# A regrouped last down group, the mixer's values ahead of its first weights, and a fourth raw weight buffer in a fp32-by-three-products encoder kernel

## The chip, the cores and the metric

The kernel runs on one core of one Trainium2 chip. The metric is the device time of one execution in microseconds (us), as the median of several runs. One core has a tensor engine (PE), a vector engine (DVE), an activation engine (ACT), GpSimd (POOL) and a sync engine (SP), which here issues most of the loads and stores. Each engine works through its own instructions in order; semaphores tie them together.

## The reference

One encoder layer over 768 tokens (a sample of 512, "S", and a prompt of 256, "P") of width 1024, in float32:

```python
x = layer_norm(a * x + 0.5 * swiglu(x, ffn1_w_gu, ffn1_w_down))
x = layer_norm(a * x + parallel_mixer(x, ...))
x = layer_norm(a * x + memory_cross_attention(x, mem, ...))
x = layer_norm(a * x + 0.5 * swiglu(x, ffn2_w_gu, ffn2_w_down))
```

`swiglu` is `(silu(x @ gate) * (x @ up)) @ down` with an inner width of 2816. The mixer projects x to a short-convolution branch, to q, k, v and gates of a bidirectional gated linear attention with four heads, to a low-rank decay, and to two sigmoid gates that merge the branches. Attention is over 256 memory rows.

## The kernel before

**Products.** Every float32 operand is split into a rounded high part (ACT, `activation` with Copy, line L87) and a low part, the source minus the high part (DVE or POOL, L88). A product is then three matmuls: high by high, low by high, high by low (L106 to L108, or L335). Weights pass through `raw` tiles (128 x 1024 float32, 512 KB), loaded by SP and split into `wh` and `wl`. The tag `raw` has three buffers in the pool `wp`, `wh` and `wl` have five each. A load into a `raw` buffer waits until the splits and sums that read its former content are done.

**Order.** The code is written against a tile layer whose scheduler places the instructions of each engine; it need not keep the order of the program text. The pools decide which instruction waits for which, since a new tile takes the buffer of an older one. So a change in the text or in a ring moves instructions elsewhere too.

**The FFN** (`ffn_fast`, twice). The inner width is 22 blocks of 128. A block needs a gate and an up weight tile, and its result, of 128 x 768, is split into a tile `hq`. FFN1 begins with two plain blocks (`front1`), FFN2 with three; the others go through `seven`: the block is a 2 x 2 product of halves, done in seven products rather than eight (a Strassen–Winograd scheme). `seven.weights` loads the two tiles `rg` and `ru` and forms four sums of their halves on DVE (tag `tt`, L312 to L320) and their splits; `seven.products` runs the seven products on the PE (psum tiles `px`, `py`, `pz`), copies three partial results out (`snap`, ACT, L340) and adds three others (`sum`, DVE, L345). The PE's next product into `px` waits for that copy or sum. Behind them, silu (ACT, L401) and the gating multiply (DVE, L402) give the hidden block. In the start of FFN1 and in the mixer, `sums` forms the activation sums S1 to S4 with four scratch tiles from the snap ring; in the mixer the rings for `tt` and `snap` are unused pieces of another tile.

**Down.** The hidden blocks are stored to DRAM (`hspill`) except the last four, and come back in pairs: a pair of inner blocks is one weight tile for each half of the output columns. A group (`down_group`) accumulates its pairs over all six token tiles in psum (`dn`) and adds the result to `acc` (DVE, L213). The last group (`down_last`) goes tile by tile, first two tiles together, then one after another, for both column halves, and each tile's layer norm (`norm`, L134 to L177) follows while the PE is at the next tile. `hr` tiles, six of them, hold the hidden blocks that come back. FFN1 has the groups [9,10,0], [1,2,3], [4,5,6] and last [7,8]; FFN2 has [9,10,0], [1,2,3], [4,5] and last [6,7,8].

**Mixer start.** After LN1 the tokens are transposed on the PE (`lt`) and split to `xh` and `xl`; `lr` is the low-rank product, `pt` the q and k projections with four weight tiles, `values(range(3))` the v projection of three token tiles (`tb`, four weight tiles from w_v), and then ten pairs go through `seven`, the first two with weights w_g, the others with w_mix. `weights_of(*pairs[0][:2])` comes before `values(range(3))` in the text.

Of the kernel before, what the change touches and what calls it, by code (L numbers as in the profile page):

```python
# [7 lines left out]
F32 = mybir.dt.float32  # L8
# [50 lines left out]
def _encoder(ctx, tc, nc, io, out, dbg):  # L59
# [21 lines left out]
    def nid(p):  # L81
        uid[0] += 1
        return f"{p}{uid[0]}"
# [181 lines left out]
    HT = TT // 2  # L265
# [11 lines left out]
        ap_ = glob["accp"].enter_context(tc.tile_pool(name="accp", bufs=1, reuse_waits="tile"))  # L277
        glob["acc"] = ap_.tile([128, 6, D], F32, name="acc")

    def seven(X, tt, snap_t, sum_t):  # L280

        unit = [None, None, 2]

        def operand(src, eng):

            if unit[2] == 2:
                unit[0] = wp.tile([128, 1024], F32R, tag="wh", bufs=5, name=nid("wh"))
                unit[1] = wp.tile([128, 1024], F32R, tag="wl", bufs=5, name=nid("wl"))
                unit[2] = 0
            c = slice(unit[2] * 512, unit[2] * 512 + 512)  # L290
            unit[2] += 1
            h, l = unit[0][:, c], unit[1][:, c]
            split(h, l, src, eng)
            return h, l

        lo, hi = slice(0, 512), slice(512, 1024)

        def weights(wg, wu):

            rg, ru = [wp.tile([128, 1024], F32, tag="raw", bufs=3, name=nid("raw")) for _ in range(2)]  # L300
            for r, w in ((rg, wg), (ru, wu)):
                if len(w.shape) == 4:
                    r4 = r[:].rearrange("p (a b c) -> p a b c", a=4, b=2)
                    for z in range(2):
                        nc.sync.dma_start(r4[:, :, z, :], w[:, :, z, :])
                else:
                    nc.sync.dma_start(r[:], w)
            V, G = nc.vector, nc.gpsimd
            t = [tt() for _ in range(4)]
            b = {}  # L310
            b["P1"] = operand(rg[:, lo], V)
            V.tensor_tensor(t[0], rg[:, lo], ru[:, lo], op=ALU.add)  # L312
            b["P5"] = operand(t[0], V)
            V.tensor_tensor(t[1], t[0], ru[:, hi], op=ALU.add)
            b["P6"] = operand(t[1], V)
            b["P3"] = operand(ru[:, hi], G)
            V.tensor_tensor(t[2], ru[:, lo], ru[:, hi], op=ALU.add)
            b["P7"] = operand(t[2], V)
            b["P2"] = operand(rg[:, hi], G)
            V.tensor_tensor(t[3], t[1], rg[:, hi], op=ALU.add)  # L320
            b["P4"] = operand(t[3], V)
            return b

        LEFT = {"P1": "A11", "P2": "A12", "P3": "S4", "P4": "A22", "P5": "S1", "P6": "S2", "P7": "S3"}

        def product(p, b, ps, start):
            tiles(X[LEFT[p]], b[p], ps, start)

        def tiles(a, w, ps, start, ks=range(4)):
            (ah, al), (wh, wl) = a, w  # L330
            for k in ks:
                c = slice(k * 128, (k + 1) * 128)
                st, sp_ = start and k == 0, k == 3
                for n, (l, r) in enumerate(((wh, ah), (wh, al), (wl, ah))):
                    nc.tensor.matmul(ps, l[:, c], r[:, k, :], start=st and n == 0, stop=sp_ and n == 2,  # L335
                                     skip_group_check=True)

        def snap(ps, nm):
            t = snap_t()
            nc.scalar.activation(t, ps, AF.Copy)  # L340
            return t

        def added(ps, t, nm):
            o = sum_t()
            nc.vector.tensor_tensor(o, t, ps, op=ALU.add)  # L345
            return o

        def products(b):

            x = psum(nid("px"))[:, :HT]  # L350
            product("P1", b, x, True)
            p1 = snap(x, "p1")
            y = psum(nid("py"))[:, :HT]
            product("P5", b, y, True)
            p5 = snap(y, "p5")
            product("P6", b, x, False)
            u2 = snap(x, "u2")
            product("P3", b, y, False)
            up1 = added(y, u2, "up1")
            product("P7", b, x, False)  # L360
            up2 = added(x, p5, "up2")
            z = psum(nid("pz"))[:, :HT]
            product("P2", b, z, True)
            g1 = added(z, p1, "g1")
            product("P4", b, x, False)
            return g1, x, up1, up2

        return operand, weights, tiles, products, (lo, hi)

    def ffn_fast(n, i, front, order6, src, groups, last):  # L370
# [7 lines left out]
        X = {}  # L378
# [6 lines left out]
        def scratch(tag, n, bufs):  # L385
            return lambda: fp.tile([128, n], F32, tag=tag, bufs=bufs, name=nid(tag))[:]

        tt, snap_t = scratch("tt", 512, 4), scratch("snap", HT, 6)
        operand, weights_of, tiles, products, (lo, hi) = seven(X, tt, snap_t, scratch("sum", HT, 4))

        def weights(j):
            return weights_of(wgu[j], wgu[NFB + j])
# [89 lines left out]
    def mixer(i):  # L482
# [72 lines left out]
        def ring(own, n):  # L555
# [7 lines left out]
        X = {nm: tuple(sa.tile([128, 4, HT], F32R, name=f"m{nm}{p}") for p in "hl") for nm in ("S1", "S2", "S3", "S4")}  # L563
        quarters(X)
        snap_t = ring(slots[4:9], HT)
        _, weights_of, _, products, _ = seven(
            X, ring(slots[0:4], 512), snap_t,
            lambda: fx.tile([128, HT], F32, tag="sum", bufs=4, name=nid("sum"))[:])

        def big(nm):  # L570
            return fx.tile([128, TT], F32, tag="big", bufs=3, name=nid(nm))
# [1 line left out]
        for k in range(4):  # L573
            a = []
            for q in (k, k + 4):
                x = big("x0")
                nc.vector.tensor_tensor(x[:], xh["all"][:, q, :].bitcast(F32), xl["all"][:, q, :].bitcast(F32),
                                        op=ALU.add)
                a.append(halves(x))
            sums(X, snap_t, k, *a)  # L580

        def w_g(c):
            return io["w_g"].rearrange("a p (b c) -> p a b c", b=2)[:, :, :, c * 128:(c + 1) * 128]

        pairs = [(w_g(2 * c), w_g(2 * c + 1), AF.Silu, silud, 2 * c) for c in range(2)]
        pairs += [(wm[16 + 2 * c], wm[17 + 2 * c], AF.Sigmoid, sigd, 2 * c) for c in range(8)]
        ws = weights_of(*pairs[0][:2])
        values(range(3))
        for n, (_, _, fn, dst, c) in enumerate(pairs):
            g1, x, u1, u2 = products(ws)  # L590
            first, second = big("first"), big("second")
# [430 lines left out]
    def front1(env):  # L1022

        X, hp, fp = env["X"], env["hp"], env["fp"]
        plain_weights, plain_block = env["plain_weights"], env["plain_block"]
        env["open_A"](("A11", "A12", "A22", "S1", "S2", "S3", "S4"))
        V, G = nc.vector, nc.gpsimd
        ip_ = ExitStack()
        ip = ip_.enter_context(tc.tile_pool(name="start", bufs=1, reuse_waits="tile"))
        X["A21"] = tuple(ip.tile([128, 4, HT], F32R, name=f"A21{p}") for p in "hl")  # L1030
        x0 = [hp.tile([128, 2, TT], F32, tag="hq", bufs=4, name=nid("x0")) for _ in range(4)]

        def part(k):
            r4 = x0[k % 4][:, k // 4, :].rearrange("p (a two b) -> p a two b", two=2, b=128)
            return r4[:, :, 0, :], r4[:, :, 1, :]

        def first(k):
            nc.sync.dma_start(x0[k % 4][:, k // 4, :], io["xT"][k, :, :])
            for nm, src in zip((("A11", "A21"), ("A12", "A22"))[k // 4], part(k)):
                put(X[nm], k % 4, src, V)  # L1040

        w0 = plain_weights(0)
        plain_block(0, w0, first)
        w1 = plain_weights(1)
        for k in range(4):
            sums(X, env["snap_t"], k, part(k), part(k + 4))
        plain_block(1, w1)
        ip_.close()
        return 2, env["weights"](2)
# [2 lines left out]
        h, l = [t[:, k, :].rearrange("p (a b) -> p a b", b=128) for t in x]  # L1052
        split(h, l, src, eng)

    def sums(X, snap_t, k, a1, a2):
        V, G = nc.vector, nc.gpsimd
        (a11, a21), (a12, a22) = a1, a2
        s_ = [snap_t().rearrange("p (a b) -> p a b", b=128) for _ in range(4)]
        V.tensor_tensor(s_[0], a22, a21, op=ALU.subtract)
        put(X["S1"], k, s_[0], V)  # L1060
        V.scalar_tensor_tensor(s_[1], s_[0], -1.0, a11, ALU.mult, ALU.subtract)
        put(X["S2"], k, s_[1], V)
        V.scalar_tensor_tensor(s_[2], s_[1], -1.0, a12, ALU.mult, ALU.subtract)
        put(X["S4"], k, s_[2], G)
        V.tensor_tensor(s_[3], a11, a21, op=ALU.subtract)
        put(X["S3"], k, s_[3], V)
# [9 lines left out]
    def front2(env):  # L1076
# [24 lines left out]
        for k in range(4):  # L1101
            x0 = hp.tile([128, 2, TT], F32, tag="hq", bufs=4, name=nid("x0"))
            for eng, s in ((nc.gpsimd, S), (nc.vector, P)):
                eng.tensor_tensor(x0[:, :, s.cols], *[d["all"][:, k:NK:4, s.cols].bitcast(F32) for d in (xh, xl)],
                                  op=ALU.add)
            a = [[x0[:, c, h * HT:(h + 1) * HT].rearrange("p (a b) -> p a b", b=128) for h in range(2)]
                 for c in range(2)]
            sums(X, env["snap_t"], k, *a)
        w3 = env["weights"](3)
        for j in range(2):  # L1110
            env["gated"](j, h01[j], nc.vector)
        env["plain_block"](2, w2)
        return 3, w3

    ffn_fast(1, 0, front1, [0, 2, 4, 1, 3, 5], io["x_tok"], ([9, 10, 0], [1, 2, 3], [4, 5, 6]), [7, 8])
    mixer(1)
    x3 = dp.tile([128, 6, D], F32, name="x3")
    with tc.tile_pool(name="lnx", bufs=1) as lp, tc.tile_pool(name="xa", bufs=1, reuse_waits="tile") as ap:
# [128 lines left out]
```

## Time and profile before

| what | value |
|---|---|
| runs shown | median 1860.47 us (1858.65 to 1863.38) |
| profiled execution | 1864.59 us |
| its span, first to last instruction | 1862.7 us |
| PE busy | 1810.8 us, 97% |
| DVE, ACT, POOL busy | 1039.0, 716.2, 616.7 us |
| mean granted clock | 0.990 |

By the trace the stages lie as follows, in us from the span's start: the first two FFN1 blocks 0 to 61, its other blocks to 341, FFN1's down groups and LN1 about 348 to 543, the start of the mixer to 612, its pairs to 758, the rest of the mixer and the cross attention to about 1356, the start of FFN2 to 1398, its blocks to 1660, its down groups and LN to the end.

How to read the lines: a group of instructions is given with its source line, its engine and its tiles (output from inputs). A wait is "engine, tile, line, releaser: total, times, longest". A window row has the busy time and the count of instructions of each engine, then the granted PE clock (1.00 is full), the share of the DMA engines and the GB/s. In a timeline row the first number is the start, the second the duration, in brackets stands the idle time before it and what ended it; "SPq" rows are DMA issues on SP's queue. Long groups share one row with "x" and their count.

### The profile page before, as it was taken

What the parts mean: (1) busy time and instruction counts of PE and PEld (TensorE: products, weight loads), DVE (VectorE), ACT (ScalarE), POOL (GpSimd) and SP (SyncE); (2) the same over time, 40 slices, a digit from 0 to 9 for tenths busy, and PEclk for the clock granted to TensorE, in tenths of its full rate; (3) what the DMA queues carried; (4) which work ended last, traced back from release to release, by engine and by line L of the source; (5) the groups of instructions that cost most, each with busy time, mean ns of one, the idle gap of its engine ahead of it and who ended that gap; (6) DMA issues with size and microseconds to landing.
All of it is one profiled execution on the core that took longest, in us unless ns stands there. A gap on an engine that the chain in (4) does not pass through costs nothing.

```text
span 1862.7 us, 25264 instructions
## 1 busy us (share of the span) xinstructions
PE 1810.8 (97%) x9902; PEld 1652.7 (89%) x9902; DVE 1039.0 (56%) x1736; ACT 716.2 (38%) x1231; POOL 616.7 (33%) x365
## 2 busy tenths in 40 slices
PE   8999999999988999999999999999999999999998
PEld 8999999988877999888888888889899999998887
DVE  8666656211395555378755853495696565641136
ACT  6444444311134454555323243335344444441111
POOL 4332332523133211622235353243543232343312
PEclk9999999999999999999999999999999999999999
DMA  4333333544331333411263262245333333327441
GB/s 166 129 129 121 119 119 102 215 170 167 118 113 34 115 132 127 142 56 35 97 224 121 70 202 80 79 162 189 110 111 129 119 120 119 119 85 265 156 150 68
DMA packets 68759, 236.85 MB, mean 127 GB/s; under 512 B 7680, under 2 KB 12032, under 8 KB 68640
## 3 DMA queue, kind: packets, MB, share of 16 engines
q1 hardware_dynamic: 63456, 220.04, 34.5%
q10 hardware_dynamic: 5184, 15.21, 2.1%
q8 instruction: 77, 1.26, 0.3%
q14 instruction: 42, 0.34, 0.1%
HBM read 189.60 MB, written 45.61 MB: 126 GB/s over the span
## 4 chain that ended last, share of the span: by engine, by line
PE 79%; DVE 13%; DMA 4%; issue 2%; ACT 1%; POOL 1%; SPq 0%; DVEq 0%; ACTq 0%; POOLq 0%
PE px L335 20%; PE py L335 9%; PE dn L108 6%; PE dn L107 6%; PE dn L106 6%; PE pt L107 4%; PE pt L106 4%; PE pt L108 4%; DMA raw<-in_ffn_gu_dram 4%; PE pz L335 4%; DVE acc L172 2%; PE to L108 2%; PE to L106 2%; PE to L107 2%; DVE rqt L143 1%
## 5 line engine op out<-in xcount | busy, mean ns | idle before, releaser
L88 POOL TENSOR_TENSOR wl<-raw,wh 128x1024 fp32r<-128x1024 f32 (+1 forms) x231 | 463.9, 2010 | 784.4 <-ACT wh L87 749.4
L87 ACT ACTIVATE wh<-raw 128x512 fp32r<-128x512 f32 (+1 forms) x309 | 259.8, 842 | 606.7 <-PE dn L108 208.0
L88 DVE TENSOR_TENSOR wl<-tt,wh 128x512 fp32r<-128x512 f32 x156 | 143.5, 921 | 112.8 <-ACT wh L87 112.7
L88 POOL TENSOR_TENSOR hq<-h,hq 128x768 fp32r<-128x768 f32 x42 | 77.9, 1855 | 306.1 <-ACT hq L87 298.6
L106 PE MATMUL pt<-xh,wh 128*128 128x512 f32 (+2 forms) x512 | 173.9, 340 | 0.0
L107 PE MATMUL pt<-xl,wh 128*128 128x512 f32 (+2 forms) x512 | 172.9, 338 | 0.0
L108 PE MATMUL pt<-xh,wl 128*128 128x512 f32 (+2 forms) x512 | 172.6, 337 | 0.0
L106 PE MATMUL dn<-wh,hr 128*128 128x512 f32 (+1 forms) x438 | 169.4, 387 | 0.0
L107 PE MATMUL dn<-wl,hr 128*128 128x512 f32 (+1 forms) x438 | 169.2, 386 | 0.0
L108 PE MATMUL dn<-wh,hr 128*128 128x512 f32 (+1 forms) x438 | 169.1, 386 | 0.0
L87 ACT ACTIVATE wh<-tt 128x512 fp32r<-128x512 f32 x156 | 97.0, 622 | 83.3 <-PE px L335 74.3
L213 DVE TENSOR_TENSOR acc<-acc,dn 128x512 f32<-128x512 f32 (+1 forms) x73 | 49.1, 676 | 135.6 <-PE dn L108 135.6
L88 DVE TENSOR_TENSOR wl<-raw,wh 128x512 fp32r<-128x512 f32 (+1 forms) x78 | 70.8, 909 | 76.2 <-ACT wh L87 76.1
L106 PEld LDWEIGHTS pt<-xh,wh 128*128 128x128 f32 x512 | 97.6, 191 | 9.9 <-issue 0.5
L108 PEld LDWEIGHTS pt<-xh,wl 128*128 128x128 f32 x512 | 97.4, 190 | 9.0
L107 PEld LDWEIGHTS pt<-xl,wh 128*128 128x128 f32 x512 | 97.6, 191 | 8.7 <-issue 0.2
L107 PEld LDWEIGHTS dn<-wl,hr 128*128 128x128 f32 x438 | 82.3, 188 | 16.7
L106 PEld LDWEIGHTS dn<-wh,hr 128*128 128x128 f32 x438 | 82.3, 188 | 16.7
L108 PEld LDWEIGHTS dn<-wh,hr 128*128 128x128 f32 x438 | 82.3, 188 | 16.6
L335 PE MATMUL px<-xh,wh 128*128 128x384 f32 x232 | 79.9, 344 | 7.2 <-DVE sum L345 6.9
L335 PE MATMUL px<-xh,wl 128*128 128x384 f32 x232 | 78.5, 339 | 0.8 <-DVE wl L88 0.8
L335 PE MATMUL px<-xl,wh 128*128 128x384 f32 x232 | 78.4, 338 | 0.0
(361 smaller groups left out, 4669.0 us busy)
## 6 DMA issues: line engine op xcount, KB each, us to landing
raw<-in_ffn_gu_dram SPq DMA_DIRECT2D x84, 512.0 KB, 3.5
hspill<-hq SPq DMA_DIRECT2D x36, 768.0 KB, 3.4
hr<-hspill SPq DMA_DIRECT2D x36, 768.0 KB, 5.5
raw<-in_ffn_dn_dram SPq DMA_DIRECT2D x44, 512.0 KB, 3.5
raw<-in_w_mix_dram SPq DMA_DIRECT2D x32, 512.0 KB, 3.4
raw<-in_w_xk_dram SPq DMA_DIRECT2D x16, 512.0 KB, 3.5
raw<-in_w_xv_dram SPq DMA_DIRECT2D x16, 512.0 KB, 3.9
raw<-in_w_xq_dram SPq DMA_DIRECT2D x16, 512.0 KB, 3.8
```

The lines of the kernel that those rows point to most:

```text
L87: nc.scalar.activation(hi, src, AF.Copy)
L88: (lo_eng or nc.vector).tensor_tensor(lo, src, hi.bitcast(F32), op=ALU.subtract)
L106: nc.tensor.matmul(o, lh, rh, start=start, stop=False)
L107: nc.tensor.matmul(o, lh, rl, start=False, stop=False)
L108: nc.tensor.matmul(o, ll, rh, start=False, stop=stop)
L143: nc.vector.scalar_tensor_tensor(t, t, -0.5, a, ALU.mult, ALU.mult)
L172: nc.vector.scalar_tensor_tensor(Ah, Ah, mv[:, 0:1], g[h][:], ALU.subtract, ALU.mult)
L213: nc.vector.tensor_tensor(A, A, ps, op=ALU.add)
L335: nc.tensor.matmul(ps, l[:, c], r[:, k, :], start=st and n == 0, stop=sp_ and n == 2, skip_group_check=True)
```

## The change

Three parts.

1. FFN1's groups become [9,10,0], [1,2,3], [4,5] and last [6,7,8], those of FFN2.
2. In the mixer, `values(range(3))` stands before the weights of the first pair.
3. `seven` gets a pool and a number `more`. Its `raw()` gives, in turn, three tiles from the common ring `raw` and one from an own buffer in that pool (the FFN's `fp`, the mixer's `fx`), so that its weights go through four buffers. For the room, in the FFN the snap ring has four tiles in place of six and the sum ring three in place of four; in the mixer the sum ring has three in place of four. `sums` takes two of its four scratch tiles from the snap ring and two from the sum ring.

```diff
-    def seven(X, tt, snap_t, sum_t):
+    def seven(X, pool, more, tt, snap_t, sum_t):
 
         unit = [None, None, 2]
+        turn = [0]
+
+        def raw():
+            turn[0] += 1
+            if (turn[0] - 1) % (3 + more) < 3:
+                return wp.tile([128, 1024], F32, tag="raw", bufs=3, name=nid("raw"))
+            return pool.tile([128, 1024], F32, tag="raw", bufs=more, name=nid("raw"))
...
-            rg, ru = [wp.tile([128, 1024], F32, tag="raw", bufs=3, name=nid("raw")) for _ in range(2)]
+            rg, ru = raw(), raw()
...
-        tt, snap_t = scratch("tt", 512, 4), scratch("snap", HT, 6)
-        operand, weights_of, tiles, products, (lo, hi) = seven(X, tt, snap_t, scratch("sum", HT, 4))
+        tt, snap_t, sum_t = scratch("tt", 512, 4), scratch("snap", HT, 4), scratch("sum", HT, 3)
+        operand, weights_of, tiles, products, (lo, hi) = seven(
+            X, fp, 1, tt, snap_t, sum_t)
...
+        def sum_t():
+            return fx.tile([128, HT], F32, tag="sum", bufs=3, name=nid("sum"))[:]
+
         _, weights_of, _, products, _ = seven(
-            X, ring(slots[0:4], 512), snap_t,
-            lambda: fx.tile([128, HT], F32, tag="sum", bufs=4, name=nid("sum"))[:])
+            X, fx, 1, ring(slots[0:4], 512), snap_t,
+            sum_t)
...
-            sums(X, snap_t, k, *a)
+            sums(X, (snap_t, sum_t), k, *a)
...
+        values(range(3))
         ws = weights_of(*pairs[0][:2])
-        values(range(3))
...
-    def sums(X, snap_t, k, a1, a2):
+    def sums(X, spare, k, a1, a2):
...
-        s_ = [snap_t().rearrange("p (a b) -> p a b", b=128) for _ in range(4)]
+        s_ = [spare[n // 2]().rearrange("p (a b) -> p a b", b=128) for n in range(4)]
...
-    ffn_fast(1, 0, front1, [0, 2, 4, 1, 3, 5], io["x_tok"], ([9, 10, 0], [1, 2, 3], [4, 5, 6]), [7, 8])
+    ffn_fast(1, 0, front1, [0, 2, 4, 1, 3, 5], io["x_tok"], ([9, 10, 0], [1, 2, 3], [4, 5]), [6, 7, 8])
```

In lists of an engine's order, before and after, the same source line has a number that is higher by 8 to 13 after the change (the load of L307 is L315), and the numbers behind tile names differ.

More of the change, by code (lines that the diff above doesn't have):

```diff
@@ L1045, in front1 @@
         for k in range(4):
-            sums(X, env["snap_t"], k, part(k), part(k + 4))
+            sums(X, (env["snap_t"], env["sum_t"]), k, part(k), part(k + 4))
         plain_block(1, w1)
@@ L1107, in front2 @@
                  for c in range(2)]
-            sums(X, env["snap_t"], k, *a)
+            sums(X, (env["snap_t"], env["sum_t"]), k, *a)
         w3 = env["weights"](3)
```

## The prediction

> **What bounds the kernel now.** I read the page first (busy time and the chain that ended last), then the PE's waits stage by stage, then windows around each wait, then the timelines of the engines that end them.
>
> ```profile
> PE 1810.8 (97%) x9902; PEld 1652.7 (89%) x9902; DVE 1039.0 (56%) x1736; ACT 716.2 (38%) x1231; POOL 616.7 (33%) x365
> PE 79%; DVE 13%; DMA 4%; issue 2%; ACT 1%; POOL 1%; SPq 0%; DVEq 0%; ACTq 0%; POOLq 0%
> ```
>
> TensorE is busy for 1810.8 of 1862.7 us, so the PE sets the end. The change removes no matmul: all it can win are gaps of the PE and the slow clock behind them. The PE's waits (engine, line, releaser: us in total, times, longest), one query each for the start of FFN1, its seven-product blocks, LN1 with the mixer's start, and FFN2's blocks:
>
> ```profile
> PE px L335 <- ACT snap L340: 4.1, 1, 4.1
> ...
> PE px L335 <- DVE sum L345: 3.5, 6, 1.1
> ...
> PE lr L517 <- DVE xl L88: 6.2, 1, 6.2
> PE tb L106 <- ACT wh L87: 3.7, 1, 3.7
> PE tb L107 <- POOL wl L88: 2.3, 1, 2.3
> PE px L335 <- DVE wl L88: 0.8, 1, 0.8
> ...
> PE px L335 <- DVE sum L345: 6.9, 7, 1.4
> ```
>
> Together 27.5 us. The windows show what follows a wait: PEclk 0.50 is half speed (columns: window, us; busy us and count of PE, PEld, DVE, ACT, POOL; PEclk, DMA share, GB/s).
>
> ```profile
> 50.69:54.74 4.05, 0.00 (x0) 0.00 (x0) 4.05 (x8) 2.42 (x5) 0.35 (x1) 0.91 0.01 2
> 54.74:60.82 6.08, 6.08 (x19) 6.08 (x20) 4.42 (x3) 1.86 (x4) 3.27 (x2) 0.50 0.58 212
> 536.94:543.16 6.22, 0.00 (x1) 0.00 (x0) 6.22 (x7) 1.06 (x1) 5.55 (x3) 0.92 0.65 197
> 543.16:548.93 5.77, 5.76 (x19) 4.72 (x19) 5.77 (x14) 0.20 (x1) 0.00 (x0) 0.50 0.51 182
> 586.13:589.89 3.76, 0.09 (x1) 0.09 (x1) 3.07 (x6) 2.37 (x4) 1.39 (x1) 1.00 0.00 0
> 589.89:596.72 6.83, 6.02 (x17) 5.23 (x18) 6.63 (x11) 2.27 (x5) 3.30 (x3) 0.50 0.24 77
> 603.54:606.96 3.42, 3.42 (x10) 2.66 (x9) 0.00 (x0) 0.00 (x0) 0.76 (x1) 0.50 0.73 254
> 612.00:758.00 146.00, 146.00 (x831) 144.22 (x830) 71.76 (x112) 70.43 (x133) 33.52 (x23) 1.00 0.37 128
> ```
>
> At half speed, busy time t does work worth t/2 at full speed, so a slow stretch loses half its busy time. The last row is the mixer's loop over the same seven products: it has no gap.
>
> **Part B: four raw buffers in the block loops.** Why do the FFN's blocks wait? The chain in FFN2:
>
> ```profile
> 1450.49 2.02 PE px L335 x12
> 1452.53 5.16 DMA raw<-in_ffn_gu_dram
> 1457.81 0.06 DVE tt L312
> 1458.42 0.69 DVE wl L88
> 1459.11 0.60 DVE tt L314
> 1459.71 0.47 DVE sum L345
> 1460.23 4.43 PE px L335 x24
> ```
>
> and POOL, then SP, just before:
>
> ```profile
> 1451.22 1.29 POOL L88 TENSOR_TENSOR wl<-raw,wh 128x512 fp32r<-128x512 f32 x1
> ...
> 1452.53 4.40 SPq L307 DMA_DIRECT2D raw<-in_ffn_gu_dram  x2
> ```
>
> The load starts at 1452.53, when POOL ends the split of the previous gate weight. With three buffers the up weight of block j+1 takes the buffer of the gate weight of block j. It arrives 5.16 us later; DVE, which runs in order, stands at L312 on it, and the sum for the PE stands behind. With four, it takes the buffer of block j−1's up weight, released a block earlier. SP's order around blocks 2 to 4 (raw is a gate or up weight, hspill the store of a finished block), before:
>
> ```order
> 14 L307 DMA raw_480<-in_ffn_gu_dram 128x1024
> 15 L307 DMA raw_623<-in_ffn_gu_dram 128x1024
> 16 L411 DMA hspill_83<-hq_281 128x1536
> 17 L307 DMA raw_624<-in_ffn_gu_dram 128x1024
> 18 L307 DMA raw_765<-in_ffn_gu_dram 128x1024
> 19 L411 DMA hspill_83<-hq_474 128x1536
> ```
>
> and now:
>
> ```order
> 14 L315 DMA raw_624<-in_ffn_gu_dram 128x1024
> 15 L315 DMA raw_480<-in_ffn_gu_dram 128x1024
> 16 L315 DMA raw_623<-in_ffn_gu_dram 128x1024
> 17 L420 DMA hspill_83<-hq_281 128x1536
> 18 L315 DMA raw_765<-in_ffn_gu_dram 128x1024
> 19 L315 DMA raw_766<-in_ffn_gu_dram 128x1024
> ```
>
> The second weight of each block now stands one place earlier, ahead of the next store. The loops wait 3.5 + 6.9 = 10.4 us. Bounds: 5 (half survives, because both loads still queue behind one store) to 10.4. The gapless mixer row is the nearest, so I take 9.6. The smaller snap and sum rings (6 to 4, 4 to 3) I cost at nothing: in this stretch the next product sum is written at 1454.76, and the gating multiplies that read the previous block's sums had ended by 1448.45, so a ring one shorter has some 6 us of cover.
>
> ```profile
> 1447.90 0.55 DVE L402 SCALAR_TENSOR_TENSOR h<-sil,sum 128x384 f32<-128x384 f32 x1
> ...
> 1454.76 0.56 DVE L345 TENSOR_TENSOR sum<-snap,py 128x384 f32<-128x384 f32 x1 [1.71 <-PE py L335]
> ```
>
> **Part A: the first seven-product block.** SP loads its gate weight at 24.52, the up weight of the next block only at 44.74, again into the buffer of an earlier gate weight; DVE's L312 waits for it:
>
> ```profile
> 44.74 1.43 SPq L307 DMA_DIRECT2D raw<-in_ffn_gu_dram  x2
> ...
> 49.89 0.69 DVE L312 TENSOR_TENSOR tt<-raw,raw 128x512 f32<-128x512 f32 x1 [3.50 <-DMA raw<-in_ffn_gu_dram]
> ```
>
> Behind it on DVE stands the gating of the plain block, then on ACT its split and the snap for which the PE waits 4.05 us. Now that load (raw_624) is early, DVE is free 3.50 us sooner, and the gap shrinks to about 0.5: 3.5 gained. The slow stretch of 6.08 us loses 3.04 of work, which goes with it: **6.5**. Bounds: 3 (a clock loss stays) to 7.1.
>
> **Part C: the last down group and LN1.** All three down matmuls of a third pair move from an accumulation over [4,5,6] to the tile-wise last group: as many matmuls, per tile 36 rather than 24. At 50.00 us for 222 (row below, FFN2, whose last group is already of three pairs) one is 0.225, so DVE gets 8.1 us a tile in place of 5.4.
>
> ```profile
> 1800.00:1850.00 50.00, 50.00 (x222) 41.39 (x222) 28.67 (x65) 8.60 (x15) 12.96 (x9) 1.00 0.25 95
> ...
> 1797.08 9.16 SPq L467 DMA_DIRECT2D hr<-hspill  x4
> ```
>
> The gap of 6.22 us ends with DVE's xl, which stands behind operations with two SBUF inputs that end where POOL's weight splits end (four splits from 531.78 to 542.49, the first behind ACT's rounding of its weight; then DVE):
>
> ```profile
> 530.63 1.06 ACT L87 ACTIVATE wh<-raw 128x1024 fp32r<-128x1024 f32 x1 [0.67 <-issue]
> ...
> 531.78 10.71 POOL L88 TENSOR_TENSOR wl<-raw,wh 128x1024 fp32r<-128x1024 f32 x4 [8.02 <-ACT wh L87]
> ...
> 527.52 0.74 DVE L172 SCALAR_TENSOR_TENSOR acc<-acc,mv,ln_g 128x512 f32<-128x512 f32 x1
> ...
> 537.54 2.76 DVE L172 SCALAR_TENSOR_TENSOR acc<-acc,mv,ln_g 128x512 f32<-128x512 f32 x1
> 540.22 2.29 DVE L142 TENSOR_TENSOR rqt<-rqy 128x1 f32<-128x1 f32 x1
> 542.43 0.68 DVE L88 TENSOR_TENSOR xl<-lt,xh 128x512 fp32r<-128x512 f32 x1
> ```
>
> L172 takes 0.74 without POOL and 2.76 beside it; even the one-column L142 takes 2.29. DVE there before (xl is what PE waits for, L172, L142 to L144 and L177 the norm of the tile before last):
>
> ```order
> 434 L172 SCALAR_TENSOR_TENSOR acc<-acc,mv_4500,ln_g_4219 128x512
> 435 L137 RECIPROCAL rqy_4506<-rqy_4506 128x1
> 436 L172 SCALAR_TENSOR_TENSOR acc<-acc,mv_4500,ln_g_4221 128x512
> 437 L142 TENSOR_TENSOR rqt_4507<-rqy_4506 128x1
> 438 L88 TENSOR_TENSOR xl<-lt_4532,xh 128x4x128
> ```
>
> and now:
>
> ```order
> 439 L143 SCALAR_TENSOR_TENSOR rqt_4495<-rqt_4495,rqa_4492 128x1
> 440 L167 BN_STATS st_4560<-acc 128x6
> 441 L144 SCALAR_TENSOR_TENSOR rqy_4494<-rqt_4495,rqy_4494 128x1
> 442 L177 SCALAR_TENSOR_TENSOR acc<-acc,rqy_4494,ln_b_4139 128x512
> 443 L177 SCALAR_TENSOR_TENSOR acc<-acc,rqy_4494,ln_b_4141 128x512
> 444 L88 TENSOR_TENSOR xl<-lt_4526,xh 128x4x128
> ```
>
> L143, L144 and two L177 now stand ahead of xl too. With 2.7 us more per tile the two L172 are done before the splits start, but these four can each be held by one of the four splits. ACT's first rounding, at 530.63, now stands behind the square root of that norm, some 2 us later by the order, so I count the splits from 533 (an estimate); three cost 3 × 10.71/4 = 8.0: xl at about 541 against 543.16, so the gap is about 4.3 and the slow clock behind it stays: **1.9**. Bounds: −2 (all four splits, a later start) to 9.1 (6.22, and 2.9 of clock).
>
> The row on L172 is what the Trainium skill, "SBUF — State Buffer", section "Who interferes with whom", states: a DVE operation with two SBUF inputs and a GpSimd operation that reads SBUF exclude each other, the later one wholly blocked. The trace agrees (2.76 beside 0.74); by that rule part C cannot be had whole while the splits run.
>
> **Part D: values before the first pair.** SP at the mixer's start, before:
>
> ```order
> 120 L96 DMA raw_4770<-in_w_mix_dram 128x1024
> 121 L305 DMA raw_5001<-in_w_g_dram 128x4x128 x2
> 122 L305 DMA raw_5002<-in_w_g_dram 128x4x128 x2
> 123 L96 DMA raw_5036<-in_w_v_dram 128x1024
> 124 L485 DMA x_4581<-acc 128x1024 x2
> 125 L96 DMA raw_5060<-in_w_v_dram 128x1024
> ```
>
> and now:
>
> ```order
> 120 L96 DMA raw_4770<-in_w_mix_dram 128x1024
> 121 L96 DMA raw_5012<-in_w_v_dram 128x1024
> 122 L494 DMA x_4581<-acc 128x1024
> 123 L96 DMA raw_5036<-in_w_v_dram 128x1024
> 124 L96 DMA raw_5060<-in_w_v_dram 128x1024
> 125 L494 DMA x_4581<-acc 128x1024
> ```
>
> The w_v loads now come ahead of the pair's w_g. Before, three of the four were issued only from 591.32, when the pair's splits had freed their buffers, and the first weight was rounded at 588.70:
>
> ```profile
> 588.70 1.05 ACT L87 ACTIVATE wh<-raw 128x1024 fp32r<-128x1024 f32 x1
> ...
> 591.32 10.99 SPq L96 DMA_DIRECT2D raw<-in_w_v_dram  x3
> ```
>
>  On the PE all 72 `tb` matmuls now follow the q/k projections, before 3 only, and then products. The PE waits here for splits (`tb` for ACT's wh 3.7, POOL's wl 2.3; `px` for wl 0.8): 6.8, and two slow stretches lose 6.02/2 + 3.42/2 = 4.7, together 11.5. The 72 matmuls last 72 × 0.225 = 16 us, in which the pair's weights are split; the first w_v weight now stands on SP right behind the q/k weights and on ACT right behind the low-rank copy, ahead of the projections' end at 586. Left is half a microsecond: **10.9**. Bounds: 6 (a wait of the 3.7 kind before `px`, its clock short) to 11.5.
>
> The Trainium skill, "TensorE: Matmul & The Clock Gate", section "What's actually happening", lets the clock fall only after an idle window of about 3.4 us. The gap of 2.3 before the stretch at 603.54 shows a fall after less; by the page that stretch would have lost nothing, and part D be 9.2 rather than 10.9. The trace differs, and the row stays in the sum.
>
> **The sum.** 9.6 + 6.5 + 1.9 + 10.9 = 28.9. The profiled span becomes 1862.7 − 28.9 = 1833.8, the profiled execution's time 1864.59 − 28.9 = 1835.7. The median of the runs shown (1860.47) lies 4.1 below it, so the forecast is 1831.6, rounded **1832**.
>
> **The rivals.** (1) *LN1 gap gone whole*: the four DVE operations slip in before the splits, xl is early, the clock stays up: 7.2 more, **1824**. For it: 2.7 us more for each tile; against: the splits' blocking. (2) *A new stall at FFN1's last group*: the hidden activations of pair 8 come late. FFN2's four such loads are issued over 9.16 us from 1797.08, the last near 1806, median 5.5 us to land, and are needed after 24 matmuls, 5.4 us: no gap there, but no slack. In FFN1 a mixer weight's load stands ahead of them on SP. Price: 1 to 5 us and 3 of clock; **1837**. (3) *The loops stay*: the store between the loads or DVE's order binds, B gives 0 to 3: **1840**. (4) *Slower*: the shorter sum ring makes DVE's product sum wait for the gating that still reads its buffer, in each of 39 blocks (20 in FFN1, 19 in FFN2), and the PE behind it. From 28.9 / 39 = 0.74 us a block the gain is eaten; at the price of one POOL split, 1.3, it is 39 × 1.3 = 51 lost: 1831.6 + 51, **1882**. Against it: the 6 us of cover. (5) *Mixer start gets a wait*: the first pair's weights, now last, hold PE with a slow clock, D only 4: **1838**.
>
> **How the numbers follow.** Forecast 0.50, (1) 0.14, (2) 0.12, (3) 0.10, (5) 0.09, (4) 0.05. The low end, 1822, takes in (1) with part A and B at their bounds; the high end, 1846, takes (2), (3) and (5), and two of them at once in part. 0.3% (5.6 us) is what a measurement can tell from no change: faster 0.93, same 0.02, slower 0.05.
>
> **What would show it.** B: no row `px <- DVE sum` above 1 us in either loop. A: the snap wait under 1 us, no 0.50 before 61. C: a wait of `lr` on xl of 3 to 5 us, with 0.50 behind it. D: no wait of `tb`, clock 1.00 to the loop. Wrong would be: a wait of `dn` in FFN1's last group, `px` on a sum in every block, or an end above 1846.

## The result

The changed kernel takes 1837.59 us (median of 4 runs, 1835.78 to 1841.17), beside 1859.56 for the kernel before on the same chip: a ratio of 0.9882, 95% interval 0.9859 to 0.9904, so 22 us faster. The forecast was 1832, range 1822 to 1846, 28.9 less. The span of the profiled execution fell from 1862.7 to 1836.1, by 26.6.

The page of the kernel after (span; busy time of the engines):

```profile
span 1836.1 us, 25283 instructions
...
PE 1799.2 (98%) x9902; PEld 1649.5 (90%) x9902; DVE 1126.4 (61%) x1737; ACT 716.2 (39%) x1231; POOL 636.1 (35%) x364
```

As many matmuls as before, but PE busy time is 11.6 less: part of the gain lies in what the records call busy. Lines of `seven` now read 8 higher (L335 is L343, L340 is L348, L345 is L353, L312 is L320).

The PE's waits after, in the same stages: the start of FFN1, its block loop, LN1 with the mixer's start, FFN2's front and blocks.

```profile
...
PE px L343 <- DVE sum L353: 1.2, 1, 1.2
PE px L343 <- ACT snap L348: 0.6, 1, 0.6
...
PE px L343 <- DVE sum L353: 1.2, 1, 1.2
PE px L343 <- ACT snap L348: 0.4, 1, 0.4
...
PE lr L526 <- DVE xl L88: 4.6, 1, 4.6
PE px L343 <- DVE sum L353: 3.0, 1, 3.0
PE px L343 <- ACT acc L348: 2.2, 1, 2.2
...
PE px L343 <- DVE sum L353: 1.2, 1, 1.2
...
PE px L343 <- ACT snap L348: 1.0, 1, 1.0
```

The first and the third row are one wait near 60, in both stages' windows (it begins at 59.8); the 1.2 of FFN2, at 1380.5, stands at the same place of its first seven-product block. Three things show at once: from there on the loops are empty of waits but for those on a copy in the last block (0.4 and 1.0), which the kernel before has too, LN1 kept three quarters of its wait, and the mixer's start has two waits that the kernel before did not have.

To see what each part gave, I took the start times of the same PE instructions in both traces and subtracted (us of the profiled executions; a product here is one of the seven, 12 matmuls):

| stretch | before | after | gained | forecast |
|---|---|---|---|---|
| A: first product into `px` to the first block's last product | 19.69 | 14.71 | 5.0 | 6.5 |
| B: FFN1's blocks, from there to the same product 18 blocks on | 268.68 | 262.18 | 6.5 | 9.6 |
| B: FFN2's blocks, first product into `px` to `dn` | 289.25 | 279.67 | 9.6 | (both) |
| FFN1's down groups, `dn` to `lr` | 183.37 | 183.35 | 0.0 | 0 |
| C: `lr`, first to last matmul | 10.02 | 8.35 | 1.7 | 1.9 |
| D: from there to the second pair's third product | 87.57 | 82.57 | 5.0 | 10.9 |
| the mixer's other pairs | 125.05 | 124.63 | 0.4 | 0 |
| the other values and the linear attention | 152.29 | 153.95 | −1.7 | 0 |
| all, with 0.1 elsewhere | | | 26.6 | 28.9 |

**The loops.** Windows over equal work, FFN1's and then FFN2's blocks, of the kernel before (us; busy us and count of PE, PEld, DVE, ACT, POOL; clock, DMA share, GB/s):

```profile
66.06:334.74 268.68, 265.11 (x1514) 261.89 (x1513) 161.73 (x250) 125.61 (x234) 83.16 (x54) 1.00 0.34 118
1398.55:1656.06 257.51, 250.91 (x1428) 247.31 (x1429) 152.81 (x236) 118.11 (x220) 78.65 (x51) 1.00 0.34 116
```

and after:

```profile
60.91:323.09 262.18, 262.18 (x1512) 262.18 (x1513) 193.01 (x248) 124.76 (x232) 89.53 (x54) 1.00 0.34 118
1381.73:1629.38 247.65, 247.65 (x1428) 247.65 (x1429) 182.82 (x234) 117.79 (x219) 84.48 (x51) 1.00 0.34 119
```

For 1428 matmuls FFN2 needed 257.51 and now needs 247.65, of which the PE is busy for all. Of the 9.9 gained only 6.6 was recorded idle time (257.51 − 250.91); 3.3 was "busy" time (250.91 − 247.65). From start to start, matmuls of 384 columns now go out every 0.173 us (247.65/1428); the record of one is twice as long (334 ns), so a pause must exceed 0.16 before it shows as idle at all. In FFN1 it is 3.6 idle and 2.9 busy of 6.5.

DVE in FFN2's blocks, grouped (count | busy us, mean ns | idle before, releaser), before:

```profile
L312 DVE TENSOR_TENSOR tt<-raw,raw 128x512 f32<-128x512 f32 x16 | 11.2, 697 | 21.1 <-DMA raw<-in_ffn_gu_dram 21.1
L314 DVE TENSOR_TENSOR tt<-tt,raw 128x512 f32<-128x512 f32 x16 | 11.0, 688 | 0.3
```

and after:

```profile
L322 DVE TENSOR_TENSOR tt<-tt,raw 128x512 f32<-128x512 f32 x16 | 31.1, 1942 | 0.6
...
L320 DVE TENSOR_TENSOR tt<-raw,raw 128x512 f32<-128x512 f32 x16 | 11.0, 685 | 0.0
```

The 21.1 us that DVE waited for the loads are gone. In return the next sum (L314, now L322) takes 1942 ns in place of 688, since it now runs earlier and beside POOL: in each of the 16, POOL is at work for 1.1 to 2.1 us of it, and before in none. That is 20 us more of DVE's time, and it costs nothing, because the PE has no gap.

**LN1.** The first row of POOL, then DVE, after:

```profile
518.79 9.84 POOL L88 TENSOR_TENSOR wl<-raw,wh 128x1024 fp32r<-128x1024 f32 x4 [17.76 <-DVE acc L172]
...
519.56 1.63 DVE L143 SCALAR_TENSOR_TENSOR rqt<-rqt,rqa 128x1 f32<-128x1 f32 x1
521.12 0.68 DVE L167 BATCH_NORM_STATS2 st<-acc 128x6 f32<-128x512 f32 x1
521.72 1.83 DVE L144 SCALAR_TENSOR_TENSOR rqy<-rqt,rqy 128x1 f32<-128x1 f32 x1
523.59 5.59 DVE L177 SCALAR_TENSOR_TENSOR acc<-acc,rqy,ln_b 128x512 f32<-128x512 f32 x2
529.10 1.27 DVE L88 TENSOR_TENSOR xl<-lt,xh 128x512 fp32r<-128x512 f32 x2
```

L143 and L144, one column each, take 1.63 and 1.83; two L177 take 5.59, and end at 529.18, just behind the last of POOL's four splits (528.63). This is the alternation of part C, row by row.

**The mixer's start.** Two windows, and in them POOL, the last step on ACT, and DVE ahead of the PE's restart at 608.29:

```profile
572.23:588.60 16.37, 16.37 (x74) 13.52 (x74) 16.34 (x24) 7.86 (x16) 4.82 (x3) 1.00 0.17 51
588.60:597.00 8.40, 6.20 (x33) 5.87 (x32) 8.40 (x15) 6.81 (x13) 8.34 (x2) 0.95 0.00 1
...
588.66 8.35 POOL L88 TENSOR_TENSOR wl<-raw,wh 128x512 fp32r<-128x512 f32 x1 [4.58 <-ACT wh L87]
...
593.42 1.30 ACT L87 ACTIVATE wh<-acc 128x512 fp32r<-128x512 f32 x2
594.63 0.47 ACT L348 ACTIVATE acc<-px 128x384 f32<-128x384 f32 x1
...
603.23 0.69 DVE L320 TENSOR_TENSOR acc<-raw,raw 128x512 f32<-128x512 f32 x1 [1.32 <-DMA raw<-in_w_mix_dram]
...
607.08 0.69 DVE L328 TENSOR_TENSOR acc<-acc,raw 128x512 f32<-128x512 f32 x1
607.69 0.55 DVE L353 TENSOR_TENSOR sum<-acc,px 128x384 f32<-128x384 f32 x1
```

The `tb` matmuls run without a gap, as foreseen. But DVE is busy for 16.34 of the 16.37 us under them, and for all of 8.40 behind them. The PE's first new wait (2.2) ends with the copy at 594.63, which stands on ACT behind roundings of the *second* pair's sums. The second (3.0) ends with a sum that stands on DVE behind L320 to L328 of the *third* pair. For that pair's second weight, landed at 603.11, DVE had its one pause, 1.32; from there to the sum it has none. POOL's split at 588.66 takes 8.35, where its kind takes 1.3, and the third pair's loads start only when it ends (597.04).

### The profile page after: what moved, and what is told of

It is laid out like the page before. It is cut to its first block, busy times and chain, and to the rows that moved or that the text cites. A ratio compares the mean times of both kernels' runs of the same rounds, so it can differ in the third digit from the quotient of the medians.

```text
span 1836.1 us, 25283 instructions
## 1 busy us (share of the span) xinstructions
PE 1799.2 (98%) x9902; PEld 1649.5 (90%) x9902; DVE 1126.4 (61%) x1737; ACT 716.2 (39%) x1231; POOL 636.1 (35%) x364
## 4 chain that ended last, share of the span: by engine, by line
PE 70%; DVE 10%; issue 1%; ACT 1%; DMA 0%; POOL 0%; DVEq 0%; ACTq 0%; POOLq 0%
PE px L343 13%; PE dn L108 6%; PE dn L106 6%; PE dn L107 6%; PE py L343 6%; PE pt L107 4%; PE pt L106 4%; PE pt L108 4%; PE pz L343 3%; PE to L108 2%; PE to L107 2%; PE to L106 2%; DVE acc L172 1%; DVE acc L177 1%; PE pp L343 1%
## 5 line engine op out<-in xcount | busy, mean ns | idle before, releaser
L88 POOL TENSOR_TENSOR wl<-raw,wh 128x1024 fp32r<-128x1024 f32 (+1 forms) x230 | 482.1, 2098 | 820.5 <-ACT wh L87 761.5
L88 DVE TENSOR_TENSOR wl<-tt,wh 128x512 fp32r<-128x512 f32 x156 | 153.3, 984 | 63.0 <-ACT wh L87 62.8
L343 PE MATMUL px<-xh,wh 128*128 128x384 f32 x232 | 77.7, 335 | 4.2 <-DVE sum L353 4.2
L343 PE MATMUL px<-xl,wh 128*128 128x384 f32 x232 | 77.5, 334 | 0.0
L343 PE MATMUL px<-xh,wl 128*128 128x384 f32 x232 | 77.5, 334 | 0.0
```

The lines of the kernel that those rows point to most:

```text
L88: (lo_eng or nc.vector).tensor_tensor(lo, src, hi.bitcast(F32), op=ALU.subtract)
```

## The experiments

Each was compared with the kernel before on the same chip.

### The parts alone

`e1_buffers` keeps only the fourth buffer with the smaller rings, `e2_values` only the order of values, `e3_group` only the groups; `e4_no_values` is the changed kernel without the order of values.

```diff
e2, against the kernel before:
+        values(range(3))
         ws = weights_of(*pairs[0][:2])
-        values(range(3))
e4, against the changed kernel:
-        values(range(3))
         ws = weights_of(*pairs[0][:2])
+        values(range(3))
```

> The kernel before with the fourth raw buffer and the smaller rings alone; groups and the order of values as before. If the parts add up as the two traces show them, FFN1's first seven-product block comes some 5 us earlier and the two block loops lose some 16 us: about 1838 (forecast of the prediction for A and B: 16.1, so 1843.5). If the fourth buffer also disturbs the mixer's start by itself (two pairs' sums and splits ahead of the first pair's snaps on DVE and ACT), the waits there grow beyond the 6.8 us of before and the time stays above 1840.

> The kernel before with values ahead of the first pair alone, three raw buffers, groups as before. Theory: the two new waits at the mixer's start after the change (2.2 on ACT's snap, 3.0 on DVE's sum) come from the fourth buffer, which lets the second pair's sums and splits stand ahead of the first pair's snaps; then this kernel has neither, and gains the forecast 10.9: about 1849. Rival: the waits belong to the values order itself (the first pair's splits fall together with the activation sums, POOL and DVE hold each other up); then it gains some 5: about 1854.5, with waits of px of some 5 us.

> The kernel before with the regrouped last down group alone. Theory: the wait of lr on xl falls from 6.2 to about 4.6 and nothing else moves: 1.7 less, about 1858. Rival: what the regroup gives is larger without the other parts, or is lost in a stall of the last group (waits of dn of 1 us or more): 1855 or above 1860.

> The changed kernel with the text order of values undone (weights of the first pair first). If the values part gives what the two traces show for the mixer's start, some 5 us, this is about 1842.5. If the fourth buffer alone already removes the waits of the start, it is not slower than the changed kernel: 1838 or less. If the order alone is worth the forecast 10.9, it is 1848.

| kernel | median us | ratio (95%) | stretch D, us |
|---|---|---|---|
| before | 1859.55 | 1 | 87.57 |
| e1: buffers | 1840.85 | 0.9896 (0.9881 to 0.9911) | 84.03 |
| e2: values | 1860.24 | 1.0000 (0.9988 to 1.0012) | 85.76 |
| e3: groups | 1859.14 | 1.0003 (0.9991 to 1.0014) | 86.93 |
| e4: buffers and groups | 1841.08 | 0.9896 (0.9881 to 0.9910) | 86.43 |
| changed: all three | 1837.59 | 0.9882 (0.9859 to 0.9904) | 82.57 |

The fourth buffer carries nearly all of it, 18.7 of 22 us. The order of values alone gives nothing that can be measured, with the others some 3.5 (1841.08 to 1837.59, from two comparisons, so rough). In stretch D the parts don't add up: the buffers alone take 3.5 off it, the order alone 1.8, buffers and groups together 1.1, all three 5.0. The groups shorten the wait of `lr` in e3 too (to 4.5 in its trace), but 1.7 us is below what these medians resolve. My theory ahead of e2, that the fourth buffer *causes* the mixer's new waits, fell: without it the wait is worse. The PE's waits of e2 there, and rows of DVE and ACT ahead of the end of the longest:

```profile
PE px L335 <- ACT acc L340: 8.8, 1, 8.8
PE lr L517 <- DVE xl L88: 6.2, 1, 6.2
PE py L335 <- DVE wl L88: 0.4, 1, 0.4
...
609.71 0.69 DVE L312 TENSOR_TENSOR acc<-raw,raw 128x512 f32<-128x512 f32 x1 [6.05 <-DMA raw<-in_w_g_dram]
...
611.64 0.63 ACT L87 ACTIVATE wh<-acc 128x512 fp32r<-128x512 f32 x1 [0.49 <-DVE acc L314]
612.18 0.47 ACT L340 ACTIVATE acc<-px 128x384 f32<-128x384 f32 x1
```

The same copy is late by 8.8: it stands behind the second pair's roundings, they behind sums on DVE that wait 6.05 for a weight, and that weight's load, with three buffers, waits for a split of the first pair (POOL ends it at 605.74, the load starts at 605.77). So the order of values by itself turns 6.8 us of three waits into 9.2 of two, and the fourth buffer relieves this.

### The smaller rings

```diff
-        tt, snap_t = scratch("tt", 512, 4), scratch("snap", HT, 6)
-        ... scratch("sum", HT, 4))
+        tt, snap_t = scratch("tt", 512, 4), scratch("snap", HT, 4)
+        ... scratch("sum", HT, 3))
```

> The kernel before with the smaller snap and sum rings (4 and 3) in both FFNs alone, three raw buffers. The prediction costs them at nothing: within 1859 +- 3, and FFN blocks of 304 to 306 and 288 to 289 us as in the runs of before. Rival: a block waits for a ring tile, but the fourth buffer more than pays for it in the changed kernel: then 1862 or more, and the fourth buffer alone would be worth more than shown.

1858.92 us, ratio 0.9995 (0.9986 to 1.0005). They cost nothing, as the prediction had it from the 6 us of cover (FFN1 from `px` to `dn` 302.72, FFN2's blocks 288.13, neither longer than in the kernel before); rival 4 has no ground.

### What bounds the mixer's start

Three mends of single suspects in the changed kernel: POOL's slow split (`e6_pair_dve`), POOL's share in the activation sums (`e7_s4_dve`), the copy's place on ACT (`e9_snap_first`).

```diff
e6:
-        ws = weights_of(*pairs[0][:2])
+        ws = weights_of(*pairs[0][:2], nc.vector)
-                ws = weights_of(*pairs[n + 1][:2])
+                ws = weights_of(*pairs[n + 1][:2], nc.vector if n == 0 else None)
e7:
-            sums(X, (snap_t, sum_t), k, *a)
+            sums(X, (snap_t, sum_t), k, *a, eng=nc.vector)
e9:
-                ws = weights_of(*pairs[n + 1][:2])
+                with tc.issue_after(p1.ins) if n == 0 else nullcontext():
+                    ws = weights_of(*pairs[n + 1][:2])
```

(`eng` replaces POOL for the low splits concerned; `issue_after` queues what it encloses on ACT behind the copy p1.)

> The changed kernel, but in the mixer's first two pairs the two low splits that stand on POOL are done by DVE. Theory: at the mixer's start POOL's split is held up by DVE's train of operations with two SBUF inputs (8.35 us for what takes 1.29 elsewhere), so a raw buffer comes free late, the third pair's weight lands late and DVE's sum for the PE stands behind it (wait of 3.0); with the splits on DVE (0.68 each) that wait is gone: about 1834, wait of px on DVE's sum under 1. Rival: DVE is the bound of this stretch by its own work, and four more operations of 0.68 lengthen it by 2.7: 1838 to 1841.

> The changed kernel, but the low parts of the mixer's activation sum S4 are split by DVE in place of POOL. Theory: DVE's chain of activation sums waits for POOL's S4 split, which stands behind the w_v splits on POOL; with it on DVE the chain runs through, the first pair's sums and the snap behind them come earlier, and the wait of 2.2 on ACT's snap goes: about 1835. Rival: the chain is bound by the rounding on ACT and the load of the weights: same as the changed kernel, 1837 to 1839.

> The changed kernel with one order fixed: on ACT, the roundings of the mixer's second pair are issued behind the first pair's first copy out of psum (snap p1), ahead of which the scheduler had put four of them. Theory: the wait of 2.2 of px on that copy comes from this order (the roundings wait for DVE's sums of the second pair); with the copy first it is gone, and the wait on DVE's sum (3.0, behind the third pair's late weight) may stay: 1834 to 1836, wait on ACT below 0.5. Rival: the copy itself is late because DVE and ACT are full to the end of the stretch; then the lost time only moves to a later product: 1837 to 1840 with waits of px of 5 in sum.

e6 gave 1839.28 (ratio 0.9886, 0.9869 to 0.9902), e7 1838.65 (0.9882, 0.9865 to 0.9899), e9 1837.74 (0.9876, 0.9858 to 0.9895): none can be told from the changed kernel (0.9882). In e6 and e7 the wait of 3.0 is gone, and the other has grown from 2.2 to 4.0 and 4.5. In e9 the copy is ahead and `px` still waits 2.5 for it, 2.9 for the sum. The wait only moved: three suspects that each stood directly ahead of a wait were not, alone, what sets the time.

Then the last experiment took work off DVE; it leaves out the eight additions, and with them the low part in the mixer's gate products:

```diff
-                x = big("x0")
-                nc.vector.tensor_tensor(x[:], xh["all"][:, q, :].bitcast(F32), xl["all"][:, q, :].bitcast(F32),
-                                        op=ALU.add)
-                a.append(halves(x))
+                a.append(halves(xh["all"][:, q, :].bitcast(F32)))
```

> The changed kernel with work left out on DVE at the mixer's start: the eight additions of high and low part (x = xh + xl, 0.95 us each, 7.6 in all) are dropped, and the mixer's activation sums are formed of the rounded high part alone; so its gate projections lose their low part, and all else stays. Theory, after the mends that only moved the wait: DVE is busy without a break from the first tb product to the second product of the pairs, and what is queued on it sets both waits of px (2.2 and 3.0). With 7.6 us less on it before that, both are gone or under 1 in sum, with the slow clock of 1.7: 1830 to 1832. Rival: POOL's splits or the raw buffers' loads set the stretch, then DVE only idles more and 4 us or more of waits stay: 1836 to 1839.

1830.10 us, ratio 0.9841 (0.9815 to 0.9866): 7.5 less than the changed kernel. Stretch D fell from 82.57 to 75.38, by 7.2, against 5.2 of waits and 1.7 of slow clock that were there. Of the PE's waits from 500 to 630 one row is left, and DVE has room in both windows:

```profile
PE lr L526 <- DVE xl L88: 4.5, 1, 4.5
...
572.00:588.60 16.60, 16.60 (x75) 13.81 (x74) 13.35 (x16) 6.54 (x12) 7.67 (x4) 1.00 0.42 128
588.60:605.00 16.40, 16.40 (x97) 16.40 (x96) 11.15 (x17) 8.56 (x16) 2.58 (x2) 1.00 0.19 64
```

So what is queued on DVE sets the mixer's start after the change, by its own time and perhaps by what it holds up on POOL. In the changed kernel's trace the eight additions take 11.4 us, since some of them run beside POOL, and without them POOL too is quicker: two of its splits for the first pair take 3.38 together, where one took 8.35. That POOL's slow split alone sets the start, e6 speaks against: with that split on DVE the PE still waited 4.0. That the additions alone are at fault does not follow; whether any other work of that length off DVE does as much was not tried.

### POOL against DVE at LN1

```diff
-            ws[b] = load_w(wm[b])
+            ws[b] = load_w(wm[b], nc.vector)
```

> The changed kernel, but the low splits of the four q/k weights, which run on POOL beside the last norms of LN1, are done by DVE. Theory: the wait of lr on xl (4.6) is all POOL against DVE: L143, L144 and L177 are held by POOL's splits, as the prediction's part C has it; with POOL idle there, xl is done before the PE gets there, the clock stays up, and it gains up to 4.6 + 2.9: 1830 to 1833. Rival: DVE's own work is the bound; four splits of about 1.3 on DVE (5.2) keep xl late: wait of 3 or more, 1836 to 1840.

1834.34 us, ratio 0.9856 (0.9841 to 0.9872). The four q/k low splits are on DVE, POOL has nothing there, and the DVE rows that took 1.63, 1.83 and 5.59 now read:

```profile
518.21 1.22 DVE L88 TENSOR_TENSOR wl<-raw,wh 128x1024 fp32r<-128x1024 f32 x1
519.34 0.15 DVE L143 SCALAR_TENSOR_TENSOR rqt<-rqt,rqa 128x1 f32<-128x1 f32 x1
...
520.01 0.15 DVE L144 SCALAR_TENSOR_TENSOR rqy<-rqt,rqy 128x1 f32<-128x1 f32 x1
520.08 0.69 DVE L88 TENSOR_TENSOR xl<-lt,xh 128x512 fp32r<-128x512 f32 x1
520.68 1.41 DVE L177 SCALAR_TENSOR_TENSOR acc<-acc,rqy,ln_b 128x512 f32<-128x512 f32 x2
```

The wait of `lr` and the slow clock behind it are gone: stretch C is 2.61 us in place of 8.35. A split of 1024 columns takes 1.22 on DVE, 2.5 on POOL beside DVE (9.84/4). The scheduler also put the first xl ahead of L177 here, so part of the earlier xl is order; the durations are the blocking itself. It agrees with the Trainium skill, "SBUF — State Buffer", section "Who interferes with whom", that a DVE operation with two SBUF inputs and a GpSimd operation that reads SBUF exclude each other.

### Mends together

> The changed kernel with the low splits of the four q/k weights on DVE and the copy ahead of the second pair's roundings; the pairs' low splits stay on POOL. If the copy's place is the cause of the mixer's first wait, this takes the 5.4 us wait that the q/k splits on DVE alone left there, and gives 1828 to 1831; if the third pair's weight behind POOL is, it stays at about 1834.

> The changed kernel with three mends together: the copy ahead of the second pair's roundings, the low splits of the first two pairs on DVE, and those of the four q/k weights on DVE. If the waits are separate, those of lr (4.6) and px (2.2 and 3.0) are all gone with their slow clock: 1826 to 1830. If DVE's work bounds the mixer's start, a wait of px of 3 to 5 stays: 1832 to 1836.

`e11_wm_snap` joins e8 and e9: 1832.92, ratio 0.9855 (0.9833 to 0.9877). `e10_all` joins e6, e8 and e9: 1829.24 (1827.52 to 1832.34), ratio 0.9835 (0.9815 to 0.9856), the fastest with the whole computation. Both keep waits of `px` and `py` of about 5.6 in sum at the mixer's start, as DVE's load there foretells, so the mends of that place gave nothing that stretch D shows (81.75 in e8 alone, 81.76 in e10). What the traces show is the gain of the q/k splits on DVE, 5.7 us of stretch C; that e10 is faster than e8 is not shown, the intervals overlap.

## Why the prediction was right, point by point

**The sum** was 28.9 against 26.6 between the profiled executions. Two terms were far off and hid each other: B was 6.5 too small (16.1 for 9.6), D 5.9 too large (5.0 for 10.9). That the sum came out near was luck in this. A was 1.5 too large, C held, and the linear attention lost 1.7 that no part of the change touches.

**Part B** failed at its upper bound. "The loops wait 3.5 + 6.9 = 10.4 us" took the sum of recorded waits for what waiting costs. The mechanism (raw load late behind POOL's split, DVE in order behind it) was right: the wait is gone with the buffer alone, in e1. The cost of a wait is its idle time and the overlap of two matmuls, and short pauses don't show as idle at all. The mixer's loop, 146.00 busy of 146, seemed to prove that busy means full speed; it too gained 0.4.

**Part A** foresaw the gap of about 0.5 (0.6 came) and that the slow clock would go (the trace has none between 16 and 527). It missed the wait of 1.2 on DVE's sum a few products later, also there in e1 (1.4).

**Part C** held in mechanism: four operations held by splits, xl done at 529.8 where the PE arrived at 525.3, 4.55 for the 4.3 forecast, the slow clock kept. e8 shows the blocking by taking it away. The size was luck in part: the forecast counted three splits from 533, 2.4 before `lr` (535.39); all four held DVE, but they began 4.9 before it (518.79 against 523.73).

**Part D** failed at "in which the pair's weights are split". I counted that there were 16 us of `tb` matmuls and not what DVE had to do in them. The rows for that were there: DVE's activation sums, the first pair's sums, and now the second pair's, in one in-order queue. The waits that it named did go; the two new ones took 7.2 back, by e12. Rival 5 (the mixer's start gets a wait, D about 4) is what happened, with 5.0, at a chance of only 0.09, though a copy and a sum held the PE and not the first pair's weights.

**Rivals.** No wait of `dn` appeared at FFN1's last group (183.35 for 183.37), so rival 2 fell, tight as the loads were. Rivals 1, 3 and 4 fell with C's wait, the empty loops and e5. Of the signs named ahead, C's came as stated, A's for the copy; B's was missed by the row of 1.2 in each first block, and D's by the clock, which was 0.50 again from 596.2.

**The median.** I carried the profiled execution's 4.1 us above the median over to the changed kernel, whose profiled execution (1837.84) lies 0.25 above its own. The surplus sat largely in the waits that the change removes: FFN2's blocks took 289.25 in that execution, but 287.60 and 287.71 in e2 and e3, whose FFN is unchanged; FFN1's stretch from `px` to `dn` 305.66, but 304.53 and 304.08. That is about 2.9 of the 4.1. Of the 6.0 between 1831.6 and 1837.59, 2.1 is the sum and 3.9 this.

## What to carry to other kernels

Price a wait by comparing the same work from start to start with a stretch that has no waits, not by the idle time in the records. When work is moved under a long run of matmuls, add up what each helper engine has queued there, in order, before calling it hidden; if mending each suspect ahead of a wait only moves the wait, take work off the engine that is never idle. When a profiled execution is slower than the median, ask in which waits the surplus lies before carrying it over.

## What was not expected of the hardware

A wait's second price, the slow clock, depends on more than its length. The linear attention has one wait on DVE before its third set of products, of 1.54 us before the change and 1.71 after. The first costs its length, the second also 3.41 us at half speed, 1.7 lost. In e1 a wait of 1.53 was followed by such a stretch, in e2 and e3 one of 1.54 by none.

All slow stretches of all traces but each trace's last, which the end cuts, are one or two times 3.41 long, and within a trace they start whole multiples of 3.413 apart (13, 156 and 170 times behind the first, in the kernel before). So the clock goes by windows that lie fixed in time. Those around the two waits, before and after:

```profile
869.78:873.19 3.41, 2.44 (x26) 2.25 (x26) 2.21 (x3) 2.62 (x5) 0.15 (x3) 1.00 0.11 43
873.19:876.60 3.41, 2.83 (x32) 2.67 (x33) 3.35 (x8) 3.04 (x7) 0.03 (x1) 1.00 0.00 0
876.60:880.01 3.41, 3.41 (x25) 3.17 (x24) 3.12 (x10) 3.33 (x5) 0.00 (x0) 1.00 0.00 0
```

```profile
852.22:855.63 3.41, 1.70 (x24) 1.51 (x22) 3.20 (x4) 2.79 (x5) 0.18 (x3) 1.00 0.03 5
855.63:859.04 3.41, 3.41 (x25) 3.09 (x22) 2.79 (x8) 2.10 (x6) 0.00 (x0) 0.50 0.00 0
```

Before, the wait falls across two windows, with 0.97 and 0.58 idle; after, it falls into one, with 1.71. With all 14 traces cut into such windows, the clock fell from full speed after each one with more than 1.84 us idle and after none with less than 1.46; in between both happened. The Trainium skill, "TensorE: Matmul & The Clock Gate", section "What's actually happening", has a free-running window of 3.413 us, which fits; that it takes one whole idle window does not, since about half a window was enough here. So a change that only shifts later work in time can win or lose 1.7 us at each such wait; in this kernel there are some five of 1.1 to 2.7 us after the mixer, in every version.
